# A hybrid encoder block in fp32 on one core: the first layer norm in a written order, grouped products, a quartered opening and a new tail

## The chip, the cores and the metric

The kernel runs on one core of one Trainium2 chip. The metric is the device time of one execution in microseconds (us), as the median of several runs. A profiled execution gives the trace that the views below read. PE is the matrix engine (TensorE) and PEld its weight loads, DVE the vector engine, ACT the scalar engine, POOL GpSimd, and SP the engine whose queue starts most transfers.

## The reference

One encoder block for 256 tokens of width 2048, in float32:

```python
proj = h @ w_in
q, k, v, r, af, ab, hy_u, gate_logits = jnp.split(proj, split_idx, axis=-1)
y_gla = _gla_branch(q, k, v, r, af, ab, ...)      # gated linear attention, both directions, 4 heads, chunks of 64
y_hy = _hyena_branch(hy_u, ...)                   # short convolution, then two long convolutions with gates
g = sigmoid(gate_logits).reshape(B, L, 2, D)
merged = g[:, :, 0, :] * (y_gla @ w_gla_o) + g[:, :, 1, :] * (y_hy @ w_hy_o)
mix = merged @ w_out
h = _layernorm(DEEPNORM_ALPHA * h + mix, ln1_g, ln1_b)
ff = jnp.square(jax.nn.relu(h @ w_ff1)) @ w_ff2   # 2048 -> 8192 -> 2048
h = _layernorm(DEEPNORM_ALPHA * h + ff, ln2_g, ln2_b)
```

The layer norm is `(x - mean) * rsqrt(var + eps) * g + b` over the 2048 channels of a token.

## The kernel before

Nearly all the work is products of a 256-token activation with weights. The weights lie in memory as 305 blocks `wblk` of 128 x 2048 floats (1 MB each), in the order in which they are used. `fetch` loads a block into one of three `raw` buffers on SP's queue. It splits each half of it (1024 columns) into a rounded high part `whi` (a cast on ACT, line 81) and the rest `wlo` (a subtraction on DVE, line 82). There are three buffers of each kind. Activations are kept in the same two parts, so a product is the sum of high x high, low x high and high x low.

There are three forms of product.

- `channel_pair` puts output channels on the partitions. For each of 16 steps (`kt`) a 512-wide product takes the high weights over both parts of the activation (line 143). Then a 256-wide one takes the low weights over the high part (line 144). The two alternate. Afterwards an ACT copy and a DVE instruction (lines 146 and 147) add the two halves of the PSUM bank. It serves 193 blocks: q, k, the Hyena inputs uv, ux and uz, the gates, the output projections go and ho, and the first MLP matrix (f0 to f3).
- `token_products` puts tokens on the partitions, with three 512-wide products per step (lines 162 to 164), in groups of four blocks and 512 output columns. It serves r, v, w_out and the second MLP matrix.
- `column_products` does the same with 256 columns at a time (lines 790 to 792), for the last group of w_out and the last group of the second MLP matrix. Before those groups `resident` loads three and four blocks and keeps them in SBUF, so that one token block (`tb`, 128 tokens) is finished ahead of the other.

A framework's scheduler orders each engine's instructions by the order of the program and by priorities. `tc.high_priority()` lifts what stands in it. Filters of the Hyena branch, GLA heads and gating are side work: `later` puts them in a list and `pump`, called after every block, issues what is due, so they run beside the products. The main products use four PSUM banks and the side work the other four.

Four places matter for the change.

- The opening. SP loads the halves of block 0 and quarters of x in turn, then the halves of block 1. Three warm-up products run first. The low-rank gate block (`pa`, lines 373 and 374) is computed alone, and q follows. ACT's queue loads the constants.
- The first layer norm, lines 762 to 776 and 826. Per token block: residual add and `bn_stats`, `norm_scale` (the inverse deviation by Ln and Exp on ACT and one Newton step on DVE), then for each of six chunks of columns an Identity on ACT (line 774), a multiplication and an addition (lines 775 and 776), and `turn`, which transposes on PE (line 826) and splits the result into `hT`. Chunk 1536 has its multiplication and addition on POOL. The first MLP block (f0, c2 = 0, c = 0) is computed by token halves (`by_tile`).
- `hy_inv`, the inverse transform of the Hyena branch. It has 12 products of 256 columns in each of 16 calls.
- The tail. Per token block of the last MLP group: sums, `norm_scale`, six chunks as above and one store for each (line 886).

These are the lines of the normalisation of a chunk and of the split:

```python
nc.scalar.activation(zc, zc, AF.Identity, scale=rs, bias=nb)
eng.tensor_tensor(zc, zc, rows[:, 0, at:at + n], op=ALU.mult)
eng.tensor_tensor(zc, zc, rows[:, 1, at:at + n], op=ALU.add)
```

Of the kernel before, what the change touches and what calls it, by code (L numbers as in the profile page):

```python
# [3 lines left out]

# [5 lines left out]
F32 = mybir.dt.float32  # L10
# [28 lines left out]

@with_exitstack  # L40
def block_kernel(
# [24 lines left out]
    MM = nc.tensor.matmul  # L66
# [19 lines left out]
    fetched = [0]  # L86
    stop_at = [W_OUT_END - 3]

    def fetch(between=lambda n, h: None):
        n = fetched[0]  # L90
        if n >= stop_at[0]:
            return
        fetched[0] = n + 1
        raw = wp.tile([P, D], F32, tag="raw", bufs=3, name=f"raw{n}")
        if n > 1:
            nc.sync.dma_start(raw, wblk[n])
        parts = []
        for h in range(2):
            if n <= 1:
                hs = slice(h * D // 2, (h + 1) * D // 2)  # L100
                nc.sync.dma_start(raw[:, hs], wblk[n][:, hs])
                between(n, h)
            hi = wp.tile([P, D // 2], F32R, tag="whi", bufs=3, name=f"whi{n}_{h}")
            lo = wp.tile([P, D // 2], F32R, tag="wlo", bufs=3, name=f"wlo{n}_{h}")
            split_hi_lo(hi, lo, raw[:, h * 1024:(h + 1) * 1024])
            parts.append((hi, lo))
        queue.append(parts)

# [24 lines left out]
    def channel_pair(act, name, dst=None, scale=1.0, by_tile=False):  # L133
        if dst is None:
            dst = base.tile([P, 2, L], F32, tag="sum", name=f"{name}_s")
        for c in range(2):
            ps = psum_main(f"{name}_{c}").rearrange("p (a b) -> p a b", a=2)
            parts = next_block()
            for ts in ((slice(0, P), slice(P, L)) if by_tile and c == 0 else (slice(0, L),)):
                for kt in range(KT):  # L140
                    hi, lo = parts[kt // 8]
                    js = slice(kt % 8 * P, (kt % 8 + 1) * P)
                    MM(ps[:, :, ts], hi[:, js], act[:, kt, :, ts], start=(kt == 0), stop=False)  # L143
# [32 lines left out]
    def rsqrt_eps(dst, src, scale, pool, name):  # L176
# [3 lines left out]
        nc.scalar.activation(t, src, AF.Ln, scale=scale, bias=eps_sb)  # L180
# [632 lines left out]
    for tb in range(NT):  # L813
        column_products(pss, mT, parts, [tb], 1)
        if tb == 1:
            fetch()
# [197 lines left out]
```

## Time and profile before

| | |
|---|---|
| time, median of 3 runs | 1891.8 us (1891.52 to 1891.81) |
| profiled execution | 1891.83 us, span 1890.0 us |
| mean granted PE clock | 0.994 |
| DMA | 375.09 MB, mean 198 GB/s over the span |
| weight blocks loaded whole (`raw<-wblk`) | 303, 4.8 us from issue to landing |
| weight splits | 596 casts on ACT of 1053 ns, 596 subtractions on DVE of 1223 ns |

Busy times are shares of the span of 1890.0 us. A line of a group gives the program's line, the engine, the operation, output and input names with shapes, the count, the busy time and the mean duration in ns of one instruction. Products are pipelined: the mean duration of a 512-wide one (389 to 399 ns) contains the time in which it overlaps its neighbours, so the cost of one in a row is the distance between two starts. A bracket at the end of a timeline line gives the engine's idle time before it and what ended that.

### The profile page before, as it was taken

To read this page: it belongs to the slowest core of one execution; us is meant where nothing else is said; L and a number is where in the kernel's file an instruction comes from. 1 tells how busy PE (TensorE), PEld (TensorE's weight loads), DVE (VectorE), ACT (ScalarE), POOL (GpSimd) and SP (SyncE) were. 2 spreads that over 40 slices of the span, in tenths; PEclk is the share of its full clock that TensorE was granted. 3 is DMA by queue.
4 is the path that set the end of the run, shared out by engine and by line. 5 is a ranking of instruction groups with operands and counts; after the bars stand their busy time and mean duration, and the time that the engine had idled before them with its cause. 6 is when DMAs were issued, how large, how long until landed. Compare 5 with 4: busy or idle time off the path is not lost.

```text
span 1890.0 us, 25333 instructions
## 1 busy us (share of the span) xinstructions
PE 1860.4 (98%) x10060; PEld 1599.7 (85%) x10060; DVE 1313.6 (70%) x1702; ACT 949.5 (50%) x1286; POOL 38.3 (2%) x60
## 2 busy tenths in 40 slices
PE   8999999999999999999999998999999999999996
PEld 7887888888888888888888888888888888888886
DVE  6787968875789888888556567666555555555556
ACT  5555556674555555555544444444434443444343
POOL 0000000000000000000000001000000000000001
PEclk9999999999999999999999999999999999999998
DMA  7667764445555555565655764555555555545552
GB/s 289 231 225 251 265 228 161 140 142 204 195 195 199 199 194 189 197 223 191 212 197 183 285 216 153 188 193 186 196 186 198 180 199 187 192 180 199 191 189 110
DMA packets 60583, 375.09 MB, mean 198 GB/s; under 512 B 7216, under 2 KB 10928, under 8 KB 20912
## 3 DMA queue, kind: packets, MB, share of 16 engines
q1 hardware_dynamic: 46512, 324.03, 47.4%
q0 software_dynamic: 5888, 29.36, 4.2%
q10 hardware_dynamic: 8064, 20.07, 3.0%
q8 instruction: 79, 1.29, 0.3%
q14 instruction: 40, 0.33, 0.0%
HBM read 356.66 MB, written 16.78 MB: 198 GB/s over the span
## 4 chain that ended last, share of the span: by engine, by line
PE 93%; DVE 4%; ACT 1%; DMA 1%; issue 1%; ACTq 0%; DVEq 0%; SPq 0%
PE f L143 13%; PE f L144 6%; PE g L143 6%; PE w L163 6%; PE w L164 6%; PE w L162 6%; PE go L143 3%; PE ux L143 3%; PE uz L143 3%; PE uv L143 3%; PE g L144 3%; PE ho L143 3%; PE ho L144 2%; PE uv L144 2%; PE ux L144 2%; PE go L144 2%
## 5 line engine op out<-in xcount | busy, mean ns | idle before, releaser
L82 DVE TENSOR_TENSOR wlo<-raw,whi 128x1024 fp32r<-128x1024 f32 x596 | 728.3, 1223 | 488.2 <-ACT whi L81 487.3
L81 ACT CAST whi<-raw 128x1024 fp32r<-128x1024 f32 x596 | 627.0, 1053 | 772.6 <-PE w L164 186.8
L143 PE MATMUL f<-hT,whi 128*128 128x512 f32 (+1 forms) x1040 | 361.7, 394 | 0.0
L144 PE MATMUL f<-hT,wlo 128*128 128x256 f32 (+1 forms) x1040 | 290.0, 279 | 0.0
L143 PEld LDWEIGHTS f<-hT,whi 128*128 128x128 f32 x1040 | 195.6, 188 | 44.3
L144 PEld LDWEIGHTS f<-hT,wlo 128*128 128x128 f32 x1040 | 197.1, 190 | 0.1
L163 PE MATMUL w<-wlo,f 128*128 128x512 f32 x480 | 186.8, 389 | 0.0
L164 PE MATMUL w<-whi,f 128*128 128x512 f32 x480 | 186.8, 389 | 0.0
L143 PE MATMUL g<-xT,whi 128*128 128x512 f32 x512 | 178.6, 393 | 0.0
L162 PE MATMUL w<-whi,f 128*128 128x512 f32 x480 | 168.0, 389 | 0.0
L144 PE MATMUL g<-xT,wlo 128*128 128x256 f32 x512 | 143.5, 281 | 0.0
L143 PEld LDWEIGHTS g<-xT,whi 128*128 128x128 f32 x512 | 95.7, 187 | 21.1
L162 PEld LDWEIGHTS w<-whi,f 128*128 128x128 f32 x480 | 90.0, 188 | 18.8
L164 PEld LDWEIGHTS w<-whi,f 128*128 128x128 f32 x480 | 90.1, 188 | 18.7
L163 PEld LDWEIGHTS w<-wlo,f 128*128 128x128 f32 x480 | 90.1, 188 | 18.5
L144 PEld LDWEIGHTS g<-xT,wlo 128*128 128x128 f32 x512 | 96.7, 189 | 0.5 <-DVE wlo L82 0.2
L143 PE MATMUL uz<-xT,whi 128*128 128x512 f32 x256 | 91.9, 398 | 0.0
L143 PE MATMUL ux<-xT,whi 128*128 128x512 f32 x256 | 91.7, 398 | 0.0
L143 PE MATMUL go<-yg,whi 128*128 128x512 f32 x256 | 91.1, 397 | 0.0
L143 PE MATMUL uv<-xT,whi 128*128 128x512 f32 x256 | 90.5, 395 | 0.0
L143 PE MATMUL ho<-yh,whi 128*128 128x512 f32 x256 | 88.8, 391 | 0.0
L144 PE MATMUL ux<-xT,wlo 128*128 128x256 f32 x256 | 72.0, 281 | 0.0
(329 smaller groups left out, 3336.7 us busy)
## 6 DMA issues: line engine op xcount, KB each, us to landing
raw<-wblk SPq DMA_DIRECT2D x303, 1024.0 KB, 4.8
Td<-T POOLq DMA_DIRECT2D x16, 768.0 KB, 4.1
Tl<-Td POOLq DMA_DIRECT2D x16, 768.0 KB, 4.5
w<-w4s ACTq DMA_DIRECT2D x16, 512.0 KB, 4.6
zr<-ln_rows ACTq DMA_DIRECT2D x4, 1024.0 KB, 10.9
raw<-wblk SPq DMA_DIRECT2D x4, 512.0 KB, 6.7
xr<-xt SPq DMA_DIRECT2D x4, 512.0 KB, 6.5
dec<-decay_in ACTq DMA_DIRECT2D x8, 256.0 KB, 3.1
```

The lines of the kernel that those rows point to most:

```text
L81: nc.scalar.copy(hi, src)
L82: nc.vector.tensor_tensor(lo, src, hi.bitcast(F32), op=ALU.subtract)
L143: MM(ps[:, :, ts], hi[:, js], act[:, kt, :, ts], start=(kt == 0), stop=False)
L144: MM(ps[:, 0, ts], lo[:, js], act[:, kt, 0, ts], start=False, stop=(kt == KT - 1))
L162: MM(pss[tb], sh, wh, start=(kt == 0), stop=False)
L163: MM(pss[tb], sh, wl, start=False, stop=False)
L164: MM(pss[tb], sl, wh, start=False, stop=(kt == KT - 1))
```

## The change

Seven parts.

1. `channel_products` replaces the loop in `channel_pair`: per half block the eight 512-wide products come first, then the eight 256-wide ones. The sums (`channel_sum`) get high priority.
2. The opening loads three blocks (the gate block and the first two of q) and x in quarters, the first quarter of block 0 and of x in halves, and computes the three in three PSUM banks, quarter by quarter. The constants are loaded from POOL's queue.
3. `hy_inv` does 6 products of 512 columns per call.
4. The splits of v get high priority.
5. The three resident blocks of w_out (174 to 176) are loaded one per group of w_out. The last group uses 512-wide `token_products`, token block 0 first.
6. The first layer norm runs in an order that the program states for PE, DVE and ACT together: `_InOrder` makes every instruction follow the one before it on its engine. POOL has no part in it. The first two MLP blocks are computed between the steps, block 0 and the first half of block 1 by token halves.
7. The tail. The multiplication by gamma moves into `add_ff`, right after the statistics are taken. Token block 0 uses 512-wide products, and DVE normalises with two instructions per chunk. For token block 1, PE adds beta and gamma times the mean's term through products with an identity and a diagonal matrix, and DVE finishes from PSUM. Neither ACT nor POOL normalises; there are four stores for the first token block and five for the second.

```diff
+class _InOrder:
...
+    def __init__(self, tc, engine):
+        self.tc, self.engine, self.last = tc, engine, None
+    def __getattr__(self, name):
+        def traced(*args, **kw):
+            ins = getattr(self.engine, name)(*args, **kw)
+            if self.last is not None:
+                dep = mybir.DependencyInfo(mybir.DependencyClass.NoSync, mybir.DependencyReason.DATA)
+                self.tc.add_manual_dep(ins.ins, self.last.ins.name, dep, reason="in order")
+            self.last = ins
+            return ins
+        return traced
 
...
+    stream = deque([*range(W_OUT_END - 3), *range(W_OUT_END, nblk - 4)])
...
-    def channel_pair(act, name, dst=None, scale=1.0, by_tile=False):
...
+        return psum_main(name).rearrange("p (a b) -> p a b", a=2)
+    def channel_products(ps, act, half, kts, ts=FULL, opens=True):
+        hi, lo = half
+        at = [(kt, slice(kt % 8 * P, (kt % 8 + 1) * P)) for kt in kts]
+        for kt, js in at:
+            MM(ps[:, :, ts], hi[:, js], act[:, kt, :, ts], start=(kt == 0 and opens), stop=False)
+        for kt, js in at:
+            MM(ps[:, 0, ts], lo[:, js], act[:, kt, 0, ts], start=False, stop=(kt == KT - 1))
+    def channel_sum(dst, ps, name, scale=1.0):
+        low = base.tile([P, L], F32, tag="low", name=name)
+        with tc.high_priority():
+            nc.scalar.activation(low, ps[:, 1], AF.Copy, scale=scale)
+            nc.vector.scalar_tensor_tensor(dst, ps[:, 0], scale, low, op0=ALU.mult, op1=ALU.add)
...
         for c in range(2):
-            ps = psum_main(f"{name}_{c}").rearrange("p (a b) -> p a b", a=2)
+            ps = channel_psum(f"{name}_{c}")
             parts = next_block()
-            for ts in ((slice(0, P), slice(P, L)) if by_tile and c == 0 else (slice(0, L),)):
-                for kt in range(KT):
-                    hi, lo = parts[kt // 8]
-                    js = slice(kt % 8 * P, (kt % 8 + 1) * P)
-                    MM(ps[:, :, ts], hi[:, js], act[:, kt, :, ts], start=(kt == 0), stop=False)
-                    MM(ps[:, 0, ts], lo[:, js], act[:, kt, 0, ts], start=False, stop=(kt == KT - 1))
-            low = base.tile([P, L], F32, tag="low", name=f"{name}_l{c}")
-            nc.scalar.activation(low, ps[:, 1], AF.Copy, scale=scale)
-            nc.vector.scalar_tensor_tensor(dst[:, c], ps[:, 0], scale, low, op0=ALU.mult, op1=ALU.add)
+            for h in range(2):
+                channel_products(ps, act, parts[h], range(8 * h, 8 * h + 8))
+            channel_sum(dst[:, c], ps, f"{name}_l{c}", scale)
...
+    OPENING = 3
+    open_ps = [channel_psum(f"open{b}") for b in range(OPENING)]
     with tc.tile_pool(name="xp", bufs=1) as xp:
...
-        fetch(load_x)
...
+        for g in range(4):
+            n = 2 if g == 0 else 1
+            for i in range(n):
+                load_w(0, g, i, n)
+                load_x(g, i, n)
+            for b in range(1, OPENING):
+                load_w(b, g, 0, 1)
+        for g in range(4):
+            pieces = 2 if g == 0 else 1
+            for b in range(OPENING):
+                if g % 2 == 0:
+                    halves_of[b] = weight_half(b, g // 2)
+                hi, lo = halves_of[b]
+                n = pieces if b == 0 else 1
+                w, step = 512 // n, 4 // n
+                for i in range(n):
+                    at = 512 * (g % 2) + w * i
+                    cs = slice(512 * g + w * i, 512 * g + w * (i + 1))
+                    split_hi_lo(hi[:, at:at + w], lo[:, at:at + w], raws[b][:, cs])
+                    if b == 0:
+                        ks = slice(4 * g + step * i, 4 * g + step * (i + 1))
+                        split_hi_lo(xT[:, ks, 0], xT[:, ks, 1], xr[g][:, step * i:step * (i + 1)])
+                channel_products(open_ps[b], xT, halves_of[b], range(4 * g, 4 * g + 4))
...
         raw = fp.tile([P, 4, P], F32, tag="w4", name="dftraw")
-        nc.scalar.dma_start(raw, dft_in)
+        nc.gpsimd.dma_start(raw, dft_in)
...
+    for c in range(2):
+        channel_sum(q_sb[:, c], open_ps[1 + c], f"q0_l{c}", 1.0 / 16.0)
+        pump()
+    for _ in range(2):
+        fetch()
...
+        with tc.high_priority():
+            for tb in range(NT):
+                split_hi_lo(vh[:, tb], vl[:, tb], pss[tb])
...
-            for tb in range(NT):
-                dst = py[:, tb * CW:(tb + 1) * CW]
-                mm3(dst, dfth[:, 2], dftl[:, 2], yh[:, tb, 0], yl[:, tb, 0], True, False)
-                mm3(dst, dfth[:, 3], dftl[:, 3], yh[:, tb, 1], yl[:, tb, 1], False, True)
             py3 = py.rearrange("p (a b) -> p a b", a=2)
+            mm3(py3, dfth[:, 2], dftl[:, 2], yh[:, :, 0], yl[:, :, 0], True, False)
+            mm3(py3, dfth[:, 3], dftl[:, 3], yh[:, :, 1], yl[:, :, 1], False, True)
...
-    def resident(slots):
...
-        for hi, lo in slots:
-            n = fetched[0]
-            fetched[0] = n + 1
+        for n, (hi, lo) in enumerate(slots, first):
...
-    def norm_scale(stats, tb, name):
...
+    x0 = tuple(ep.tile([P, D], F32R, tag=t, name=t) for t in ("xh", "xl"))
+    slots = [x0] + halves(ep, "f", "wr1")
+    parts = []
     for g in range(3):
         pss = token_group(mT, f"wo{g}")
         for tb in range(NT):
             add_mix(pss[tb], tb, g * 512, 512)
-    x0 = tuple(ep.tile([P, D], F32R, tag=t, name=t) for t in ("xh", "xl"))
-    parts = resident([x0] + halves(ep, "f", "wr1"))
-    pss = [[psum_main(f"wo3_{tb}{ch}") for ch in range(2)] for tb in range(NT)]
-    column_products(pss, mT, [queue.popleft()], range(NT), 0)
-    stop_at[0] = nblk
+        parts += resident(slots[g:g + 1], W_OUT_END - 3 + g)
+    pss = [psum_main(f"wo3_{tb}") for tb in range(NT)]
+    token_products(pss, mT, [next_block()], range(NT), 0)
     hT = act_tile(ep, "hT", "hT")
-    for tb in range(NT):
-        column_products(pss, mT, parts, [tb], 1)
-        if tb == 1:
-            fetch()
-        with tc.high_priority():
-            for ch in range(2):
-                add_mix(pss[tb][ch][:, 0:256], tb, 1536 + ch * 256, 256)
-            rs, nb = norm_scale(st1, tb, "1")
-
-        def turn(at, n):
-            pt = psum_side(f"ht{tb}_{at}")
-            k0 = at // P
-            for k in range(n // P):
-                nc.tensor.transpose(pt[:, k * P:(k + 1) * P], z1[:, tb, (k0 + k) * P:(k0 + k + 1) * P], ident)
-            dst = [hT[:, k0:k0 + n // P, i, tb * P:(tb + 1) * P] for i in range(2)]
-            split_hi_lo(dst[0], dst[1], pt[:, 0:n].rearrange("p (a b) -> p a b", b=P))
-
-        for at, n in CHUNKS:
-            norm_chunk(z1, rows1, tb, at, n, rs, nb)
-            if at < 1536:
-                turn(at, n)
-        turn(1536, 512)
+    first = [channel_psum(f"f0_0_{c}") for c in range(2)]
+    fblocks = [next_block() for _ in range(2)]
+    CHUNKS = ((0, 256), (256, 256), (512, 512), (1024, 512), (1536, 512))
+    norm, turned = {}, {}
+    def center(tb, c):
+        at, n = CHUNKS[c]
+        zc = z1[:, tb, at:at + n]
+        rs, nb = norm[tb]
+        eng.scalar.activation(zc, zc, AF.Identity, scale=rs, bias=nb)
+    def affine1(tb, c):
+        at, n = CHUNKS[c]
+        zc = z1[:, tb, at:at + n]
+        eng.vector.tensor_tensor(zc, zc, rows1[:, 0, at:at + n], op=ALU.mult)
+        eng.vector.tensor_tensor(zc, zc, rows1[:, 1, at:at + n], op=ALU.add)
+    def hi_lo(tb, c):
+        at, n = CHUNKS[c]
+        k0, k1 = at // P, (at + n) // P
+        return [hT[:, k0:k1, i, tb * P:(tb + 1) * P] for i in range(2)]
+    def turn(tb, c):
+        at, n = CHUNKS[c]
+        pt = psum_side(f"ht{tb}_{at}")
+        for k in range(n // P):
+            cs = slice(at + k * P, at + (k + 1) * P)
+            eng.tensor.transpose(pt[:, k * P:(k + 1) * P], z1[:, tb, cs], ident)
+        turned[tb, c] = pt[:, 0:n].rearrange("p (a b) -> p a b", b=P)
+        eng.scalar.copy(hi_lo(tb, c)[0], turned[tb, c])
+    def low_part(tb, c):
+        hi, lo = hi_lo(tb, c)
+        eng.vector.tensor_tensor(lo, turned[tb, c], hi.bitcast(F32), op=ALU.subtract)
+    def products(tb, k4):
+        ts = slice(tb * P, (tb + 1) * P)
+        for c in range(2 if k4 < 2 else 1):
+            channel_products(first[c], hT, fblocks[c][k4 // 2], range(4 * k4, 4 * k4 + 4), ts,
+                             opens=(c == 0 or tb == 0))
+    in_order(True)
+    token_products(pss, mT, parts, [0], 1)
+    add_mix(pss[0], 0, 1536, 512)
+    norm[0] = norm_scale(st1, 0, "1")
+    for c in range(5):
+        center(0, c)
+    for c in range(3):
+        affine1(0, c)
+    token_products(pss, mT, parts[0:2], [1], 1)
+    for c in range(2):
+        turn(0, c)
+        low_part(0, c)
+    token_products(pss, mT, parts[2:3], [1], 3)
+    turn(0, 2)
+    affine1(0, 3)
+    add_mix(pss[1], 1, 1536, 512)
+    norm[1] = norm_scale(st1, 1, "1", lambda: low_part(0, 2))
+    products(0, 0)
+    turn(0, 3)
+    center(1, 0)
+    center(1, 1)
+    affine1(0, 4)
+    low_part(0, 3)
+    products(0, 1)
+    turn(0, 4)
+    low_part(0, 4)
+    for c in range(2, 5):
+        center(1, c)
+    products(0, 2)
+    products(0, 3)
+    affine1(1, 0)
+    turn(1, 0)
+    affine1(1, 1)
+    turn(1, 1)
+    low_part(1, 0)
+    affine1(1, 2)
+    turn(1, 2)
+    low_part(1, 1)
+    products(1, 0)
+    low_part(1, 2)
+    affine1(1, 3)
+    turn(1, 3)
+    products(1, 1)
+    low_part(1, 3)
+    affine1(1, 4)
+    turn(1, 4)
+    products(1, 2)
+    low_part(1, 4)
+    products(1, 3)
+    in_order(False)
+    channel_products(first[1], hT, fblocks[1][1], range(8, KT))
...
-            r = channel_pair(hT, f"f{qi}_{c2}", by_tile=(qi == 0 and c2 == 0))
+            if qi == 0 and c2 == 0:
+                r = base.tile([P, 2, L], F32, tag="sum", name="f0_0_s")
+                for c in range(2):
+                    channel_sum(r[:, c], first[c], f"f0_0_l{c}")
+            else:
+                r = channel_pair(hT, f"f{qi}_{c2}")
...
                 nc.vector.bn_stats(st2[:, tb, at // 256 + i, :], zc[:, i * 256:(i + 1) * 256])
+            nc.vector.tensor_tensor(zc, zc, rows2[:, 0, at:at + n], op=ALU.mult)
...
-    parts = resident(halves(ep, "f", "wr2") + halves(ep, "hT", "wr3"))
-    pss = [[psum_main(f"w2_33_{tb}{ch}") for ch in range(2)] for tb in range(NT)]
-    for tb in range(NT):
-        column_products(pss, fts[3], parts, [tb], 0)
-        with tc.high_priority():
-            for ch in range(2):
-                add_ff(pss[tb][ch][:, 0:256], tb, 1536 + ch * 256, 256, 3)
-            rs, nb = norm_scale(st2, tb, "2")
-        for at, n in CHUNKS:
-            norm_chunk(z1, rows2, tb, at, n, rs, nb)
-            nc.sync.dma_start(out[tb * P:(tb + 1) * P, at:at + n], z1[:, tb, at:at + n])
+    parts = resident(halves(ep, "f", "wr2") + halves(ep, "hT", "wr3"), nblk - 4)
+    def affine(tb, at, n, rs, nb):
+        zc = z1[:, tb, at:at + n]
+        t = ep.tile([P, 512], F32, tag="aff", bufs=1, name=f"aff{tb}_{at}")[:, 0:n]
+        nc.vector.scalar_tensor_tensor(t, rows2[:, 0, at:at + n], nb, rows2[:, 1, at:at + n], op0=ALU.mult, op1=ALU.add)
+        nc.vector.scalar_tensor_tensor(zc, zc, rs, t, op0=ALU.mult, op1=ALU.add)
+    def store(tb, at, n):
+        nc.sync.dma_start(out[tb * P:(tb + 1) * P, at:at + n], z1[:, tb, at:at + n])
+    ps = psum_main("w2_33_0")
+    token_products([ps], fts[3], parts, [0], 0)
+    pss = [psum_main(f"w2_33_1{ch}") for ch in range(2)]
+    add_ff(ps, 0, 1536, 512, 3)
+    rs, nb = norm_scale(st2, 0, "2")
+    for at in range(0, D, 512):
+        affine(0, at, 512, rs, nb)
+        store(0, at, 512)
+    column_products([None, pss], fts[3], parts, [1], 0)
+    BIASED = ((256, 512), (768, 512), (1280, 512), (1792, 256))
+    po = {}
+    for at, n in BIASED:
+        po[at] = psum_side(f"lo{at}")[:, 0:n]
+        tc.keep_in_program_order(MM(po[at], ident, rows2[:, 1, at:at + n], start=True, stop=False))
+    for ch in range(2):
+        add_ff(pss[ch][:, 0:256], 1, 1536 + ch * 256, 256, 3)
+    rs, nb = norm_scale(st2, 1, "2")
+    dg = ep.tile([P, P], F32, tag="dg", name="dg")
+    nc.vector.tensor_scalar(dg, ident, nb, None, op0=ALU.mult)
+    affine(1, 0, 256, rs, nb)
+    store(1, 0, 256)
+    for at, n in BIASED:
+        MM(po[at], dg, rows2[:, 0, at:at + n], start=False, stop=True)
+        zc = z1[:, 1, at:at + n]
+        nc.vector.scalar_tensor_tensor(zc, zc, rs, po[at], op0=ALU.mult, op1=ALU.add)
+        store(1, at, n)
```

More of the change, by code (lines that the diff above doesn't have):

```diff
@@ L3 @@
 from contextlib import ExitStack
+from types import SimpleNamespace
 import concourse.bass as bass
@@ L364, in block_kernel @@
         later(n + 2, filt_freq(c, o))
-    pa = psum_main("pa").rearrange("p (a b) -> p a b", a=2)
-    fetch()
-    parts = next_block()
-    for kt in range(KT):
-        hi, lo = parts[kt // 8]
-        js = slice(kt % 8 * P, (kt % 8 + 1) * P)
-        MM(pa, hi[:, js], xT[:, kt], start=(kt == 0), stop=False)
-        MM(pa[:, 0], lo[:, js], xT[:, kt, 0], start=False, stop=(kt == KT - 1))
+    pa = open_ps[0]
     nc.scalar.copy(a_low, pa[:, 1])
```

105 lines of the change are left out of this document (53 added, 52 removed).

## The prediction, made before the changed kernel had run

> **What bounds the kernel now.** I read the page's first and fourth parts, then the timeline, the groups and the table of stretches at five places the change touches.
>
> ```profile
> PE 1860.4 (98%) x10060; PEld 1599.7 (85%) x10060; DVE 1313.6 (70%) x1702; ACT 949.5 (50%) x1286; POOL 38.3 (2%) x60
> PE 93%; DVE 4%; ACT 1%; DMA 1%; issue 1%; ACTq 0%; DVEq 0%; SPq 0%
> ```
>
> PE is the bound nearly everywhere. Time can be won only where PE waits (opening, first layer norm, tail), where it does fewer or wider products, or where a product costs less. The stretches (us, busy time with count for PE, PEld, DVE, ACT, POOL; then granted clock, DMA share, GB/s):
>
> ```profile
> 5.60:9.00 3.40, 0.78 (x2) 0.00 (x0) 1.24 (x2) 2.09 (x2) 0.00 (x0) 1.00 1.02 388
> 9.10:12.40 3.30, 2.13 (x7) 1.84 (x8) 2.95 (x3) 2.37 (x3) 0.00 (x0) 0.50 1.05 390
> 12.50:15.80 3.30, 3.30 (x12) 2.81 (x11) 2.97 (x3) 2.62 (x3) 0.00 (x0) 0.50 0.99 394
> 550.00:900.00 350.00, 350.00 (x2057) 307.16 (x2057) 312.16 (x375) 190.64 (x270) 14.15 (x26) 1.00 0.55 201
> 1159.40:1162.70 3.30, 1.82 (x17) 1.68 (x15) 2.35 (x10) 2.21 (x4) 0.34 (x1) 1.00 0.00 0
> 1162.80:1166.10 3.30, 0.71 (x4) 0.29 (x2) 3.07 (x3) 1.70 (x5) 2.63 (x2) 0.50 0.00 0
> ```
>
> The opening is short of data and at half clock; the Hyena input stage has DVE 89% busy (312.16 of 350); in the layer norm PE idles and the clock halves after a stretch that was 1.82 of 3.30 us busy.
>
> **Unit prices**, from distances between starts at full clock: a 512-wide product 0.227 us (token groups), a 256-wide one 0.120 (column products), a transpose 0.109. A pair of the channel products (512 then 256) costs 0.3467 in gates f0, f1, but about 0.353 in f2, f3. The groups show it in two 60 us stretches, 1440 to 1500 and 1240 to 1300:
>
> ```profile
> L143 PE MATMUL f<-hT,whi 128*128 128x512 f32 x171 | 60.5, 399 | 0.0
> ```
> ```profile
> L143 PE MATMUL f<-hT,whi 128*128 128x512 f32 x175 | 60.7, 391 | 0.0
> ```
>
> Over all 3088 pairs (193 blocks of 16) the excess over 0.3467 adds to 8.3 us, 3.4 of it in f2, f3.
>
> **1. Grouping.** Eight 512-wide, then eight 256-wide products, the same number. 0.227 + 0.120 is already 0.3467, so only the excess can go. If it is lost where the width changes, two changes per half instead of sixteen leave an eighth: 7.3 won. If not, 0. Alternating f0 and f1 lose nothing, so the width change is not the whole cause; token and column runs, of one width, stay at 0.227 and 0.120, which speaks for runs. I take 5 (0 to 8.3). The low part is wanted 8 x 0.227 = 1.8 us after the high part, which eases DVE.
>
> **2. Opening.** The first product waits for the x split:
>
> ```profile
> 10.27 0.79 PE L373 MATMUL pa<-xT,whi 128*128 128x512 f32 x1 [3.89 <-DVE xT L82]
> ```
>
> Block a ends at 18.5 and the third block at 29.7, without side products. I laid the quartered loads along the measured landing of bytes (about 195 GB/s up to 5.5 us, then 390), splits at 0.61/0.68 us for 512 columns and 1.05/1.22 for 1024 (ACT/DVE). First product 6.1, third block ends at 25.2 at full clock; at 26.6 with half clock up to 12.5; at 28.2 with half clock up to 15.9. The stretch up to 9.0 again has PE busy for less than two thirds, so I take 26.2: 3.5 won (0.5 to 6.7). The low end has block 3 late: its buffer comes free at about 18.5, a 1024 KB load lands 4.8 later, and cast and split put its first products at 24.5 to 26. On POOL's queue now stand nine constant loads, the first of which waits for the x buffers; the filters that need them start some two blocks later, beside products: 0, and a microsecond if a filter product then stands at PE's head.
>
> **3. Fewer, wider products.** hy_inv: 16 x (12 x 0.120 - 6 x 0.227) = 1.25. Last group of w_out: 192 x 0.120 - 96 x 0.227 = 1.25. Token block 0 of the last MLP group: 96 x 0.120 - 48 x 0.227 = 0.6. Together 3.1. The resident loads moved ahead on SP's queue cost 0: ACT idles 1.67 us before each cast of that stage.
>
> **4. First layer norm.** PE's gaps, from the timeline:
>
> ```profile
> 1155.12 1.11 PE L826 MATMUL ht<-ident,zr 128*128 128x128 f32 x6 [0.84 <-DVE zr L776]
> 1162.52 0.99 PE L826 MATMUL ht<-ident,zr 128*128 128x128 f32 x4 [1.48 <-DVE zr L776]
> 1166.54 0.87 PE L826 MATMUL ht<-ident,zr 128*128 128x128 f32 x3 [3.03 <-DVE zr L776]
> ```
>
> From 1130 to 1190 PE takes 59.84 us for work that is 51.33 by the unit prices: 8.5 lost. The written order, laid out by hand with the rows' durations (add 0.6, aggregate to scale 1.4, centre 0.70, affine 2 x 0.6 for 512 columns), leaves 4.8 idle. Its largest gap, 1.9, is before the transposes of the second token block's third chunk: ACT runs three centres ahead of the copy that DVE's low part needs, and token block 1's first products stand behind on PE. On ACT the two row loads for the second norm wait for the last affine step, with the last copy into hT behind them; that is in the layout. The second half block done by tokens costs 8 x 0.12 more. So 8.5 - 4.8 - 1.0 = 2.7. If the 1.9 gap drops the clock for 6.8 us, as it lasted here (1162.8 to 1169.6), some 2.2 go. I count two thirds of that: 1.3 won (-1 to 4).
>
> That stretch of 1159.40 is what makes me count it. The Trainium skill ("TensorE: Matmul & The Clock Gate", What's actually happening) says the gate closes after an idle window of about 3.4 us; by that a 1.9 us gap costs nothing and this term would be 2.7. The trace disagrees: 1.82 us of work in such a window did not hold the clock.
>
> **5. Tail.**
>
> ```profile
> 1875.64 0.42 DVE L855 TENSOR_TENSOR zr<-zr,w 128x256 f32<-128x256 f32 x1 [1.69 <-PE w L792]
> 1878.35 3.49 ACT L774 ACTIVATE zr<-zr,lnb,lrs 128x256 f32<-128x256 f32 x6 [0.86 <-DVE lnb L766]
> 1884.50 0.74 DVE L776 TENSOR_TENSOR zr<-zr 128x256 f32<-128x256 f32 x2
> ```
>
> The last product ends at 1875.60, the span at 1889.97: 14.4 us. After: sums, statistics and the extra gamma multiply to 3.6, the diagonal matrix 3.9, then four products in turn with DVE's multiply-add (0.68 each); last of these done at 7.5, its store landed by 10.3, end 11.6. The fp32 products are not in the trace; the nearest are the warm-up ones, two records of 0.85 us each. Won 2.7; 0.4 if they run at half clock (3.5 at best, if they cost no more than a 0.227 row).
>
> **6. Priorities.** The v splits go first: PE waits of 0.58, 0.86 and 1.09 us near 296, 323 and 353 may shrink or move; 0 (-2 to 2).
>
> Sum: 5 + 3.5 + 3.1 + 1.3 + 2.7 = 15.6. The profiled execution took 1891.83 (span 1890.0 and 1.8 around it), equal to the median of 1891.8: **1876.2 us**. Adding the terms' deviations as independent ones gives 1870 to 1883 for this case alone.
>
> **Rivals.**
> A, the pace stays: the excess comes back with grouped products. For: f0, f1 alternate without loss, so alternation may not be the cause. 1876.2 + 5 = 1881.2.
> B, the clock: half clock to 15.9 in the opening (2.0 less), the full drop in the layer norm (2.3 less), the tail's products at half (2.3 less): 1882.8. For: the stretches 9.10 and 12.50 stand at 0.50 though PE was 2.13 and 3.30 busy.
> C, slower: the sums, now of high priority, go ahead of the split of the next low weights on DVE. In the Hyena input stage DVE idles 11%, 0.30 us per half block of 2.77, and a sum takes 0.42. It decides where low weights come later than 1.8 us after the high ones; then each of about 63 blocks from v to uz loses up to 0.42: 26 us, 1902. Against: PEld idles only 0.4 to 0.5 us in that stage for the low weights, so they are now well ahead.
> D, the clock holds in the layer norm although PE has the 1.9 gap: 1.4 better, 1874.8. Against: the 1159.40 stretch. This is the time that the page's rule gives.
>
> **How the numbers follow.** Forecast 0.53, A 0.17, B 0.08, C 0.13, D 0.09. The range 1867 to 1888 holds the forecast's bounds, A, B and D with little left out; C lies outside. About 0.2% (3.8 us) is what a measurement can tell from no change. Faster by more: the forecast, D, and most of A and B, 0.83; within it, their upper ends, 0.04; slower, C, 0.13.
>
> **What would show it.** Grouping: pairs at 0.3467 in f2, f3. Opening: third block ended by 26.2. Layer norm: PE's gaps add to 4.8 with one of 1.9 and the clock at 0.50 behind it. Tail: last product to end of span 11.6. Wrong if PE waits for low weights in the stages uv, ux, uz, or if PE's sum of waits elsewhere grows by more than 4 us.

## The result and the profile after

The changed kernel takes 1883.0 us (median of 4 runs, 1882.1 to 1883.1) against 1891.7 for the kernel before: 8.7 us less, ratio 0.9949 with a 95% interval from 0.9937 to 0.9961. The profiled execution took 1882.98 us with a span of 1881.2. The forecast was 1876.2 in a range from 1867 to 1888. The sign and the range held, and little more than half of the gain came.

Parts 1 and 4 of the page after:

```profile
PE 1862.4 (99%) x9852; PEld 1594.2 (85%) x9852; DVE 1313.7 (70%) x1709; ACT 948.2 (50%) x1278; POOL 30.8 (2%) x61
PE 95%; DVE 2%; ACT 1%; DMA 1%; issue 0%; SPq 0%; DVEq 0%; ACTq 0%
```

PE has 208 instructions fewer and its share of the last chain rises from 93% to 95%. DVE's falls from 4% to 2%, ACT's stays at 1%. Where the time went is seen from when PE starts each stage (us, from the records of the first product of a stage; "lead" is before less after):

| | before | after | lead |
|---|---|---|---|
| k | 66.94 | 63.86 | 3.1 |
| v | 259.79 | 253.58 | 6.2 |
| gates, first half (g) | 367.42 | 359.72 | 7.7 |
| Hyena input (uv) | 472.64 | 473.72 | -1.1 |
| w_out (wo) | 1065.34 | 1064.70 | 0.6 |
| second MLP matrix (w) | 1345.00 | 1342.28 | 2.7 |
| end of span | 1889.97 | 1881.20 | 8.8 |

A lead of 7.7 us turns into a lag of 1.1 within the first gates: that stage takes 114.0 us instead of 105.2. The forecast had no such loss.

**The gates.** PE's timeline of the changed kernel from 376 us. The line at 384.12 is the start of the third block of the gates:

```profile
377.40 0.49 PE L93 MATMUL o<-vh,sth 128*128 128x512 f32 x1 [1.30 <-ACT sth L108]
...
384.12 2.93 PE L93 MATMUL g<-xT,whi 128*128 128x512 f32 x8 [3.69 <-DVE vl L109]
```

The chain of waits shows what PE stood behind:

```profile
380.38 0.69 DVE gm L509
381.07 1.18 DVE gb L514 x2
...
382.30 1.18 DVE gb L516 x2
383.48 0.59 DVE vl L109
```

The third gate block needs a PSUM bank that the last v group still holds. That group ended at 359.7, but its split writes `vh` and `vl`, of which there is one buffer, and head 2's output products still had to read the old ones. They come on PE at 377.4, after two gate blocks. Then the split's low part stands on DVE behind the scans of head 3's gates (`gb`). In the kernel before, the same output products began at 375.7, 8.3 us after the gates' first product; after, 17.7 us. The side work had not gained what PE had.

The wait has a second price. Behind it the clock is halved for 3.4 us, which is about 1.7 us more:

```profile
385.15:388.56 3.41, 3.41 (x14) 3.02 (x13) 3.41 (x11) 2.61 (x6) 0.00 (x0) 0.50 0.00 0
```

**Why the side work is late.** The first lines are from the timeline of the changed kernel from 0 to 62 us:

```profile
22.44 0.54 POOL L308 DMA_DIRECT2D dftraw<-dft_in  x1 [18.41 <-DVE xT L109]
...
37.27 0.70 PE L93 MATMUL mlp<-emb_sb,mlpw 33*128 33x256 f32 x2
```

The constants that wait for the x buffers are issued at 22.4 to 24.0 us, instead of 15.9 to 17.2, and the last lands at 33.7 instead of 22.8. The filter network starts at 37.3 instead of 28.8, the first filter products at 69.9 instead of 61.3, and head 0's gates at 283.7 instead of 278.2, although v starts 6 us earlier.

**The opening.** The stretches after, at the places shown of before:

```profile
5.60:9.00 3.40, 2.75 (x10) 1.44 (x8) 0.93 (x2) 0.62 (x1) 0.00 (x0) 1.00 0.88 210
9.10:12.40 3.30, 2.16 (x10) 1.81 (x11) 2.03 (x3) 1.86 (x3) 0.00 (x0) 1.00 1.01 371
12.50:15.80 3.30, 1.83 (x11) 1.46 (x11) 2.31 (x3) 2.00 (x3) 0.00 (x0) 1.00 1.04 395
```

The clock stays at 1.00, which was the good end of the forecast. The data do not: 210 GB/s from 5.6 to 9.0, where 388 moved before. The second and third blocks' first quarters land at 9.55 and 10.23. PE's timeline from 5.9 us:

```profile
10.24 2.12 PE L93 MATMUL open<-xT,whi 128*128 128x512 f32 x8 [1.64 <-ACT whi L108]
...
14.77 1.20 PE L93 MATMUL open<-xT,whi 128*128 128x512 f32 x4 [1.47 <-DVE xT L109]
...
27.48 2.00 PE L93 MATMUL q<-xT,whi 128*128 128x512 f32 x8
```

The third block ends at 27.5.

**The pace.** The groups of f0, f1 (1240 to 1300) and of f2, f3 (1440 to 1500):

```profile
L93 PE MATMUL f<-hT,whi 128*128 128x512 f32 x173 | 43.4, 392 | 0.0
```
```profile
L93 PE MATMUL f<-hT,whi 128*128 128x512 f32 x172 | 43.2, 392 | 0.0
```

173 and 172 products in 60 us, where there were 175 and 171: the fast stage has become slower and the slow one faster. The starts of single products say why. In ho the first five steps of a run of 512-wide products last 233, 236, 228, 233 and 231 ns and the others 226.7; the first 256-wide step lasts 113 ns and the others about 120. That is 20 ns for every half block, in all 32 runs of ho alike.

**The layer norm**, from PE's timeline, and two stretches:

```profile
1159.62 0.74 PE L49 MATMUL f<-hT,whi 128*128 128x256 f32 x4 [0.39 <-DVE hT L49]
1161.30 0.41 PE L49 MATMUL ht<-ident,zr 128*128 128x128 f32 x2 [0.30 <-DVE zr L49]
1163.33 1.05 PE L49 MATMUL ht<-ident,zr 128*128 128x128 f32 x4 [1.63 <-DVE zr L49]
```
```profile
1159.60:1162.90 3.30, 1.79 (x12) 1.34 (x12) 2.91 (x7) 2.11 (x4) 0.00 (x0) 1.00 0.00 0
1163.00:1166.30 3.30, 2.97 (x14) 3.00 (x15) 1.78 (x4) 0.59 (x1) 0.00 (x0) 0.56 0.02 5
```

The longest gap stands where the layout by hand had it, before the third chunk of token block 1, and the clock drops behind it. Counted from the unit price of the products before it, as the layout counts, it is 1.8 us; the bracket says 1.63, since the profile lets a product end later than its price.

**The tail**, from the timeline:

```profile
1869.89 3.17 PE L93 MATMUL lo<-zr,ident 128*128 128x512 f32 x8
...
1874.02 3.27 PE L93 MATMUL lo<-zr,dg 128*128 128x512 f32 x8 [0.96 <-DVE dg L1040]
```

From the start of the last weight product (1869.77) to the end of the span (1881.20) it is 11.4 us, against 14.65 before.

### The profile page after: what moved, and what is told of

It is laid out like the page before. It is cut to its first block, busy times and chain, and to the rows that moved or that the text cites. A ratio compares the mean times of both kernels' runs of the same rounds, so it can differ in the third digit from the quotient of the medians.

```text
span 1881.2 us, 24912 instructions
## 1 busy us (share of the span) xinstructions
PE 1862.4 (99%) x9852; PEld 1594.2 (85%) x9852; DVE 1313.7 (70%) x1709; ACT 948.2 (50%) x1278; POOL 30.8 (2%) x61
## 4 chain that ended last, share of the span: by engine, by line
PE 95%; DVE 2%; ACT 1%; DMA 1%; issue 0%; SPq 0%; DVEq 0%; ACTq 0%
PE f L93 19%; PE w L93 19%; PE g L93 9%; PE uv L93 5%; PE go L93 5%; PE ho L93 5%; PE uz L93 5%; PE ux L93 5%; PE r L93 5%; PE v L93 4%; PE wo L93 4%; PE k L93 2%; PE q L93 2%; PE Zp L93 1%; PE yp L93 1%; PE s L93 1%
## 5 line engine op out<-in xcount | busy, mean ns | idle before, releaser
L109 DVE TENSOR_TENSOR wlo<-raw,whi 128x1024 fp32r<-128x1024 f32 (+2 forms) x603 | 729.1, 1211 | 467.3 <-ACT whi L108 451.0
L108 ACT CAST whi<-raw 128x1024 fp32r<-128x1024 f32 (+2 forms) x603 | 627.3, 1041 | 765.2 <-PE w L93 188.5
L93 PE MATMUL w<-whi,f 128*128 128x512 f32 x960 | 296.2, 389 | 0.0
L93 PE MATMUL f<-hT,whi 128*128 128x512 f32 x1000 | 250.7, 392 | 0.0
L93 PEld LDWEIGHTS f<-hT,wlo 128*128 128x128 f32 x1000 | 136.3, 190 | 9.7
L93 PE MATMUL f<-hT,wlo 128*128 128x256 f32 x1000 | 139.5, 282 | 0.0
L93 PE MATMUL r<-whi,xT 128*128 128x512 f32 x256 | 82.3, 391 | 0.0
L93 PE MATMUL v<-whi,xT 128*128 128x512 f32 x256 | 79.7, 390 | 0.0
L93 PE MATMUL g<-xT,wlo 128*128 128x256 f32 x512 | 72.6, 284 | 0.0
L93 PE MATMUL wo<-whi,mT 128*128 128x512 f32 x208 | 64.2, 389 | 0.0
## 6 DMA issues: line engine op xcount, KB each, us to landing
zr<-ln_rows ACTq DMA_DIRECT2D x4, 1024.0 KB, 10.9
```

The lines of the kernel that those rows point to most:

```text
L93: return eng.tensor.matmul(*args, **kw)
L108: nc.scalar.copy(hi, src)
L109: nc.vector.tensor_tensor(lo, src, hi.bitcast(F32), op=ALU.subtract)
```

## Experiments

All were run beside the kernel before, in three groups, each on another chip. The kernel before took 1892.3, 1893.2 and 1894.1 us in the three, so a run is set against one of another group by its ratio. The changed kernel itself was run again in the third:

> The changed kernel itself beside the others on the same chip: 1882 to 1884, so that the differences to it are read from one chip.

It took 1883.9 us (1880.8 to 1886.1), ratio 0.9946 (0.9932 to 0.9960). Its spread goes with the clock: the fastest execution had a mean granted clock of 1.000, the slowest of 0.996. In the profiled one PE's gap before 14.88 us was 2.4 us, the clock went to 0.50 behind it, and the third block ended at 29.1 instead of 27.5. The waits in the gates and in the layer norm were those of the first execution, but behind them the clock held. The gates took 112.5 us instead of 114.0.

The traces show one reason for such differences. In the profiled executions the changes of the clock lie whole multiples of 3.413 us apart (in the changed kernel at 385.15, 388.56, 1163.38 and 1166.80). Here are the stretches of that grid around the gap of the layer norm. The first is the changed kernel's, the others are the repeat's, counted on from its change at 15.02 us:

```profile
1159.97:1163.38 3.41, 1.48 (x13) 1.06 (x12) 3.05 (x7) 1.74 (x4) 0.00 (x0) 1.00 0.00 0
```
```profile
1158.48:1161.90 3.42, 2.36 (x18) 1.77 (x16) 2.85 (x7) 3.01 (x6) 0.00 (x0) 1.00 0.00 0
1161.90:1165.31 3.41, 2.16 (x20) 2.19 (x20) 2.28 (x5) 0.62 (x2) 0.00 (x0) 1.00 0.02 5
```

In the repeat a grid point splits the gap, and no stretch has PE busy for less than 2.16 us. The busy share alone is not the rule: in the repeat's gates the clock held behind stretches with 1.51 and 1.60 us, and in the kernel before it fell behind one with 1.93 (1159.35 to 1162.76).

**Constants that wait for nothing.**

```diff
-        mw = fp.tile([P, 3, P], F32, tag="mlpw", name="mlpw")
+        mw = cp.tile([P, 3, P], F32, tag="mlpw", name="mlpw")   # cp: a pool of its own, opened before xp; so mc, et
```

> The changed kernel, with the three small constants of the filter network (322 KB) in space of their own, so that their loads do not wait for the x buffers. Theory 1: these loads, issued at 22.4 to 24.0 us and landed by 33.7, made the filters and then the GLA heads start about two blocks late; so the output products of head 2 came on PE only where the third gate block already wanted the PSUM bank of the last v group, and PE stood 1.46 and 3.85 us. Then the heads come a block earlier, both waits go, and the time falls by 4 to 6 us to 1877 to 1879. Theory 2: the high priority of the v splits made the waits; then the time stays at 1883 within 1 us.

1880.7 us, ratio 0.9936 (0.9924 to 0.9949). The first filter products come earlier in PE's order, and the waits shrink but stay:

```profile
PE g L93 <- DVE vl L109: 2.6, 1, 2.6
```

The wait for `sth` is gone, and the one for the bank falls from 3.7 to 2.6 us.

**The v splits at normal priority.**

```diff
-        with tc.high_priority():
-            for tb in range(NT):
-                split_hi_lo(vh[:, tb], vl[:, tb], pss[tb])
+        for tb in range(NT):
+            split_hi_lo(vh[:, tb], vl[:, tb], pss[tb])
```

> The changed kernel with the v splits at normal priority as before. Theory 1 (late constants): head 2's output products stay where the third gate block waits, the PE waits near 376 and 380 stay, 1883 within 1 us, or up to 2 us more since the v stage had lost its waits. Theory 2 (v priority): the waits near 380 go, 1878 to 1879.

1880.7 us, ratio 0.9936 (0.9924 to 0.9949). In the profiled executions the v stage is 2.2 us shorter than with the high priority (104.0 against 106.1, and 106.1 in the repeat), but the gates are not (113.8), and the wait for the bank is still 3.0 us. So the high priority cost some 2 us by the trace; the intervals of the ratios overlap. Neither cause alone was the whole. Both move the output products of head 2 a little, and neither far enough.

**All side work earlier.** The five small constants that nothing needs early go behind the large one on POOL's queue, on top of the early constants:

```diff
+        for d in free[1:]:                       # loads of ba, conv, mask, sgn, ident
+            tc.add_manual_dep(d.ins, last.ins.name, dep, reason="behind")   # last: load of dftraw
```

> The kernel of the early constants, with the five small constants that nothing needs early (rows of 12 to 768 bytes) put behind the large one on POOL's queue. Theory 1: those five loads held the opening's data back (213 GB/s from 5.6 to 9.0 us against 388 before); then the quarters land up to 2 us earlier and the third block ends by 25.7 instead of 27.5; and head 2's output products, which now stand 2 us of products after the last v group instead of 11, end PE's wait of 2.7 us in the gates: 1876 to 1877. Rival: the pieces of 1 and 2 KB per partition are what load slowly; the opening stays at 27.5 and only the wait in the gates goes: 1878.

1877.0 us, ratio 0.9911 (0.9893 to 0.9928). Filter products now start at 57.1 us and head 0's gates at 270.5. PE's timeline from 355 us:

```profile
363.46 1.99 PE L93 MATMUL g<-xT,whi 128*128 128x512 f32 x8
...
366.72 0.40 PE L93 MATMUL o<-vh,sth 128*128 128x512 f32 x1
...
377.61 0.63 PE L93 MATMUL g<-xT,whi 128*128 128x512 f32 x2
```

The output products stand 3 us behind the gates' first product, and the third block starts with no bracket: no wait. The gates take 102.4 us, and the stage uv starts at 465.9, 7.8 us earlier than in the changed kernel. This settles the gates. On the opening the rival was right: the third block ends at 27.1.

**The queue of the constants.**

```diff
-        nc.gpsimd.dma_start(raw, dft_in)
+        nc.scalar.dma_start(raw, dft_in)          # and the other eight
```

> The changed kernel with its constants loaded from ACT's queue again, at the same places of the program, so that the filters keep their late place. It tells what the move to POOL's queue did for the opening. Theory 1: loads from POOL's queue beside SP's made the data come slowly up to 10 us (234 to 262 GB/s against 381 to 403 before); then the first quarters of the second and third block land before 9 us instead of 9.6 and 10.2 and the opening ends earlier, by up to 2 us: 1881 to 1882. Theory 2: with ACT's loads among SP's, SP waits for earlier loads before its fifth one; the opening ends later than 27.5 us and the time is 1884 or more. The waits near 376 and 380 stay in both.

1883.9 us, ratio 0.9947 (0.9933 to 0.9960), no different. The first quarters of the second and third block land at 7.94 and 9.60 instead of 9.55 and 10.23, but the stretch from 6 to 10 us moves 246 GB/s against 240, and the third block ends at 27.2. The slow loading belongs to neither queue. What makes it is open. It is not the size of the pieces alone, since pieces of the same 2 KB per partition moved at 395 GB/s from 12.5 to 15.8 us.

**Grouping undone, and grouping alone.**

```diff
         for kt, js in at:
             MM(ps[:, :, ts], hi[:, js], act[:, kt, :, ts], start=(kt == 0 and opens), stop=False)
-        for kt, js in at:
             MM(ps[:, 0, ts], lo[:, js], act[:, kt, 0, ts], start=False, stop=(kt == KT - 1))
```

> The changed kernel with the 512-wide and 256-wide channel products alternating again. Theory A: the runs of eight cost a start-up of about 20 ns per half block (first five 512-wide steps 233, 236, 228, 233 and 231 ns in place of 226.7, the first 256-wide one 113 in place of 120), 386 x 0.020 = 7.8 us, which takes back the 8.3 that grouping saves: 1883 within 1.5 us. Theory B: grouping gave the forecast 5 us and something else lost them: 1888.

1899.0 us, ratio 1.0033 (1.0022 to 1.0044): slower than the kernel before. Both theories were far off. The groups of this kernel from 1240 to 1300:

```profile
L93 PE MATMUL f<-hT,whi 128*128 128x512 f32 x171 | 60.5, 399 | 0.0
```

f0 and f1, which alternated without loss in the kernel before (x175), run here at the slow pace, and so does ho. I call a step of PE a wait when it is over 0.15 us above the unit price, and count the rest as excess. At full clock the excess of the channel products over 0.227 and 0.120 adds to 22.1 us here, 13.4 in the kernel before and 11.4 in the changed one. The alternation has two paces, 0% and 1.9% over the sum. The kernel before had the good one in ho, f0, f1 and a part of the gates. Another 7 us are PE's waits (23.5 against 16.7 in the changed kernel, without the warm-up and the tail's fp32 products). About half of them stand in the r stage (3.7 against none), where r follows the channel stages, and most of those are for low weights:

```profile
PE r L93 <- DVE wlo L109: 2.0, 4, 0.6
```

The other way round, grouping alone in the kernel before:

> The kernel before with nothing changed but the order of the channel products: runs of eight per half block (the lone gate block of the opening stays alternating). Theory A: the run start-up of 20 ns per half block, 384 x 0.020 = 7.7 us, takes the place of the alternating excess; no wait for low weights stood in the channel stages of this kernel, so 1891 to 1892, no change. Theory B: grouping is worth the forecast 5 us here and the changed kernel lost them elsewhere: 1887. Theory C: it is worth the 16 us that undoing it cost in the changed kernel: 1876.

1888.8 us (1887.6 to 1889.6) against 1893.2, ratio 0.9975 (0.9966 to 0.9984): 4.4 us by the medians, 4.7 by the ratio. Theory B has the size, but not for its reason: the excess falls only from 13.4 to 10.9, and the rest is in PE's waits, which fall from 14.5 to 12.7. ho, f0 and f1 pay 0.7% where they paid nothing, and f2, f3 pay 0.7% where they paid 1.9%.

**Longer runs.**

```diff
-            for h in range(2):
-                channel_products(ps, act, parts[h], range(8 * h, 8 * h + 8))
+            # all sixteen 512-wide products of the block, then all sixteen 256-wide ones
```

> The changed kernel with sixteen 512-wide products of a whole block and then sixteen 256-wide ones. Theory A: half as many changes from 256 to 512, so 193 x 0.020 = 3.9 us less: 1879, with the same first five steps and 226.7 from the sixth to the sixteenth. Theory B: the excess belongs to the 512-wide channel products at whatever place (mean 4 ns each): 1883.

1880.9 us, ratio 0.9933 (0.9921 to 0.9946). The excess falls from 11.4 to 7.7 us, near the 3.9 forecast, and ho, f0 to f3 pay 0.36% instead of 0.7%. So the cost is the start of a run. The time falls by less. The gates wait 0.6 us longer, and the clock was at half longer: for 17.1 us in the opening, the gates and the layer norm of the profiled execution, against 6.8 in the changed kernel's.

**Everything together.**

> The moved constants and runs of sixteen together. If both causes are rightly read: 3.9 us from half as many run starts, head 2's output products 8 us of products ahead of the last v group's end so that no bank of the gates waits: 1872 to 1873. If the waits in the gates come from elsewhere: 1876.

1880.1 us, ratio 0.9926 (0.9908 to 0.9943): slower than the moved constants alone. The waits of PE from 245 to 425 us:

```profile
PE v L93 <- DVE wlo L109: 4.2, 3, 2.0
PE yt L617 <- DVE rs L226: 2.4, 1, 2.4
```

The waits have moved from the gates into v, where PE now waits for DVE's splits of the weights. That the heads, which come earlier, hold DVE up there is the likely reason; it was not tested alone. Too early costs about as much as too late.

So the long runs were kept out of every stage up to the gates:

```diff
+            run = 8 if name[0] in "qk" or name.startswith("g1") else 16
```

> The moved constants (1877.0) and runs of sixteen only from the Hyena input stage on, so that no instruction up to the gates changes its place. Run starts saved: the 140 blocks of uv, ux, uz, go, g2, ho, f0 to f3 less the two of the layer norm, 2.8 us at 20 ns each: 1874. If the loss of the kernel with everything (1880) was not the early GLA heads but the long runs: 1877 or more.

1874.1 us, ratio 0.9894 (0.9881 to 0.9908), as expected.

**The layer norm's order.** First without the stated order:

```diff
-    in_order(True)
+    in_order(False)
```

> The changed kernel with the stated order of the first layer norm left out: the same instructions, ordered by the scheduler (it puts both token blocks' transposes together and the first MLP products behind them). Theory 1: the stated order is what shortens PE's gaps (3.3 us of waits over 0.2 us from 1149 to 1165 in the changed kernel); without it PE waits again 6 us or more, with the clock halved: 1885 to 1887. Rival: two token blocks finished apart and no work on POOL are the gain, and the order adds nothing: 1883.

1883.3 us, ratio 0.9944 (0.9929 to 0.9960), the same as the changed kernel. PE's timeline of this kernel:

```profile
1154.85 0.74 PE L93 MATMUL f<-hT,whi 128*128 128x256 f32 x4 [0.70 <-DVE hT L906]
1162.98 0.63 PE L900 MATMUL ht<-ident,zr 128*128 128x128 f32 x4 [1.40 <-DVE zr L888]
1164.18 0.72 PE L900 MATMUL ht<-ident,zr 128*128 128x128 f32 x4 [0.58 <-DVE zr L888]
```

The scheduler's order has a gap of much the same size at the same chunk. The stated order of this change adds nothing by itself. Another stated order does:

```diff
     products(0, 1)
+    affine1(1, 0)
     turn(0, 4)
     low_part(0, 4)
-    for c in range(2, 5):
-        center(1, c)
+    turn(1, 0)
+    affine1(1, 1)
+    center(1, 2)
     products(0, 2)
+    turn(1, 1)
     products(0, 3)
...
+    low_part(1, 0)
+    center(1, 3)
+    low_part(1, 1)
+    affine1(1, 2)
+    products(1, 0)
+    turn(1, 2)
+    center(1, 4)
+    affine1(1, 3)
+    low_part(1, 2)
     turn(1, 3)
```

> The kernel of the late runs of sixteen with another stated order in the layer norm: the affine steps of token block 1 start before the last transposes of token block 0 are split, and the centres stand between the copies instead of ahead of them. By the durations laid out by hand PE's gaps fall from 4.8 to 3.3 us and the longest from 1.9 to 1.0: 1.5 us less, 3 if the clock then holds, 1871 to 1872.5. Rival: DVE is the bound of this stage whatever the order, as the scheduler's own order was as fast: 1874, no change.

1870.8 us (1870.2 to 1871.2), ratio 0.9877 (0.9864 to 0.9891): the fastest, 23.3 us under the kernel before and 13.1 under the changed one on the same chip. Two stretches of its layer norm, the first with the longest gap, and the wait there:

```profile
1147.50:1150.90 3.40, 2.34 (x19) 1.91 (x19) 3.22 (x8) 1.67 (x3) 0.00 (x0) 1.00 0.00 0
1151.00:1154.40 3.40, 3.25 (x29) 3.01 (x27) 2.84 (x5) 1.20 (x3) 0.00 (x0) 1.00 0.00 0
```
```profile
1149.12 0.41 PE L49 MATMUL ht<-ident,zr 128*128 128x128 f32 x2 [0.76 <-DVE zr L49]
```

From f's first product to w's first it is 187.1 us against 190.4 in the kernel with the late runs of sixteen. The longest wait, counted from the unit prices, is 0.9 and no longer 1.8 us. The clock is the other difference. The kernel of the late runs, behind its gap:

```profile
1154.20:1157.50 3.30, 3.30 (x16) 3.30 (x17) 1.71 (x4) 0.59 (x1) 0.00 (x0) 0.50 0.02 5
1157.60:1160.90 3.30, 3.30 (x19) 3.30 (x19) 1.14 (x3) 1.23 (x2) 0.00 (x0) 0.56 0.00 0
```

The repeat of the changed kernel, which has the old order and kept its clock there, tells the two apart. From the first transpose to the first 512-wide product of the MLP it takes 20.0 us, the kernel of the late runs 21.7 and this one 18.4. So 1.7 of these 3.3 us are the clock and 1.6 are the order. Waits over 0.15 us add to 4.7 us in the repeat and 3.1 here: the layout had 4.8 and 3.3. Its 1.5 us came, and so did the rest that it promised if the clock held. The rival fell.

## Why the prediction was right or wrong

The sum of the steps was 15.6 us and the profiled executions differ by 8.9.

- **Grouping** (5 forecast). Right in size for the kernel before (4.7 measured alone), but the step's reason fell. The width change is a cost at the start of a run, 20 ns per half block or 7.8 us in all, which nearly eats the 8.3 of excess it removes; this is rival A's mechanism. By all steps of the channel products 2 to 2.5 us of excess go. Some 2 us more lie in PE's waits, mostly for DVE, which the prediction named as easier and priced at nothing. That the two add up to the forecast is luck. Undone in the changed kernel, grouping is worth 15 to 16 us. The profiled executions are 17.5 apart: 10.7 because alternation then has its slow pace nearly everywhere, and 6.8 in waits. What sets the pace of an alternating stage stays open.
- **Opening** (3.5). 2.2 came (29.7 to 27.5), inside the bounds; the upper one, 6.7, has no row behind it, since 25.2 at full clock is 4.5. I had taken the landing curve of the kernel before for the new loads, and that was the term that was mis-sized. The clock, where I had counted a loss, held in that execution and fell in another.
- **Constants on POOL's queue** (0, or 1 us). This is the step that failed. I saw that they wait for the x buffers and that the filters start two blocks later, and stopped at "beside products: 0". The cover was gone 300 us later: the side work holds a PSUM bank and the only v buffers that the gates need, at 5.3 us in two waits (1.46 and 3.85 from the unit price, 1.30 and 3.69 in the brackets), and the half clock behind them cost about 1.7 more in that execution. With the side work early again these waits are gone, and the time is 6 us less (ratio 0.9911 against 0.9949).
- **Fewer, wider products** (3.1). By the distances between starts, without steps over 0.35 us, the products of hy_inv fall from 23.1 to 22.2 us, those of w_out from 88.3 to 87.2 and those of the second MLP matrix from 349.4 to 348.9: 2.5 together. A little less than forecast, mostly in hy_inv, whose 512-wide products take 0.231 us in their short runs.
- **Layer norm** (1.3). The 1.9 us gap came at 1.8, at its place, and the clock dropped, but for 3.4 us and not for 6.8. From w_out's first product to w's first it is 2.1 us less. 1.1 of that is w_out's wider products, and f0 and f1 lose about 1.1 to the starts of runs, so some 2 is the layer norm's. Whether it is more or less is the clock's luck: the same stretch, 277.6 us here, took 277.1 in the repeat, where the clock held, and 278.8 in the kernel of the early constants, where it was halved for 6.8 us. Right in size, but not by the stated order, since the scheduler's order is as fast.
- **Tail** (2.7, end 11.6 after the last product). 3.2 less. The fp32 products take 0.857 us for 512 columns (two records of 0.428): half of what the warm-up rows show, as the sum took it.
- **Priorities** (0, -2 to 2). The v splits cost some 2 us, at the edge of the bound. The sign was not foreseen. The waits in v did shrink, from 2.5 to 0.4 us; why the stage still takes longer than without the priority stays open.

The prediction's second sign of being wrong, waits elsewhere that grow by more than 4 us, did not show, though its failed step did. PE's waits grew from 1.4 to 6.9 us in the gates, but r and v lost 3.4, so the sum grew by 2.1.

Of the rivals, C did not occur: the stage uv, ux, uz has no PE wait above 0.15 us. Waits for low weights show in the alternating kernel, in r; whether the sums cause them was not tested. The time lies beside B's 1882.8, but by chance: of B's three terms only a part of the drop in the layer norm came. B also counts that drop too high, 2.3 us where two thirds of 2.2 already stood in the forecast. D did not occur in this execution and did in the repeat. Of ten profiled executions with this order the clock fell behind the gap in nine and held in one. From the first transpose to the first 512-wide product of the MLP it took 20.0 us with the clock held, 20.4 with a drop of 3.4 us and 21.7 with one of 6.8, so the 2.2 of the prediction was too much. The Trainium skill ("TensorE: Matmul & The Clock Gate", What's actually happening) lets the clock fall after an idle window of about 3.4 us; here a stretch of 3.41 us in which PE was busy for 1.48 was enough. Some 0.7 of that are transposes; whether they count like products no run here tells.

## What to carry to other kernels

Work "beside the products" has a due time: when its start is moved, follow its chain to the first buffer or PSUM bank that the main stream needs back, however much later, and price the wait there. When a kernel alternates two product widths, measure the pace stage by stage, and prefer long runs of one width, but change their place only where no side work is timed by it. A stated order is worth something where it shortens and splits the gaps: here about half of the gain was the shorter waits and half the clock that held. That it is stated is worth nothing. Before crediting an edit with a microsecond or two, look whether the clock fell in both executions.

## What the runs showed of the hardware

- A run of 512-wide products behind 256-wide ones needs five steps of 228 to 236 ns before it settles at 226.7, and the first 256-wide step behind 512-wide ones takes 113 ns instead of 120 (all 32 runs of ho). Runs of sixteen halve the cost.
- Alternating 512 and 256 wide has two paces, 346.7 and about 353 ns a pair, that last through whole stages and change from kernel to kernel though the stage's products keep their order (ho, f0 and f1: 346.7 in the kernel before, 353.3 in the alternating one).
- In the opening the loads moved 208 to 291 GB/s from 6 to 10 us (stretches of 2 us) in the quartered openings looked at, whichever queue carried the constants, and 324 to 417 from there to 18 us; the kernel before had 381 and 403 from 6 to 10.
- The clock changes at points of a grid of 3.413 us. A gap of 1.8 us was followed by half clock, for one or two stretches of the grid, in nine of ten profiled executions, and not in the tenth, whose two stretches had PE busy for 2.36 and 2.16 us. With gaps of at most 0.9 us in the layer norm the mean granted clock was 1.000 in all four executions.
